# A two-layer trunk on one core of Trainium2: three of seven out-projection operands kept as plain values, weight differences in order of use, conditioning loads tied to their pairs

## The chip, the cores and the metric

The kernel runs on one core of a Trainium2 chip. A core has five engines with a queue of instructions each: TensorE (PE) multiplies matrices, VectorE (DVE), ScalarE (ACT) and GpSimd (POOL) work on tiles, SyncE (SP) here only starts DMA transfers. Each queue runs in its order; engines wait for one another through semaphores. The order within a queue is fixed when the program is built, by a scheduler that places the instructions by readiness and by the order in which the code emits them. The metric is the device time of one execution in microseconds, as the median of repeated runs.

## The reference

A trunk of two layers on 1024 positions of width 1024, fp32. Layer 0 mixes by gated DeltaNet and stick-breaking attention, layer 1 by retention; each mixer and each SwiGLU feed-forward has an RMS norm, modulated by rows that are computed from a conditioning vector (adaLN). What the change touches is the last two of these:

```python
for l in range(DEPTH):
    mod = (c_act @ ada_w[l] + ada_b[l])[:, None, :]
    sh_m, sc_m, gt_m, sh_f, sc_f, gt_f = jnp.split(mod, 6, axis=-1)
    h = rms_norm(x, norm_mix[l]) * (1 + sc_m) + sh_m
    ...
    x = x + gt_m * y
    h = rms_norm(x, norm_ffn[l]) * (1 + sc_f) + sh_f
    gu = h @ ffn_w_in[l]
    g, u = gu[..., :2816], gu[..., 2816:]
    x = x + gt_f * ((silu(g) * u) @ ffn_w_out[l])
```

## The kernel before

Activations are held transposed, as eight tiles of 128x1024 in fp32 (`xs`). A product of two fp32 matrices is made of three TensorE products: each operand is split into a high part (`hi`, a cast on ACT) and a low part (`lo`, value minus `hi`, a subtraction on DVE or POOL), and hi·hi, lo·hi and hi·lo are summed.

**The seven-product scheme.** `wino` (L1280) computes a pair of 128-wide output blocks by the Strassen–Winograd scheme: seven products in place of eight. The activation side has the operands A11, A12, A22, S1, S2, S3, S4 (quarters of the input and sums of them), the weight side B11, B21, B22, T1, T2, T3, T4. One product is 12 matmuls of 128x512 (4 slices of the contraction, three for hi and lo). `main` runs the pairs; in each the order of the products is A11·B11 (`m1`), S2·T2 and S3·T3 (`m67`), S1·T1 (`m5`), A22·T4 (`m4`), A12·B21 (`m2`), S4·B22 (`m3`). After each product the function `step(n, nm)` of the caller runs, which emits other work there. The weights of a pair come as two raw tiles of 128x1024 by SP (`w_load`, L127, two buffers). `prep_a` splits the first (L1297, L1298); `prep_b` (L1303–1327) makes the differences on the raw tiles in place (L1317, L1318, L1321, L1322) and splits B22, T2, T1, T3, T4 (L1319/1320, L1325/1326). Sums of the results are made at L1378–1398. The scheme serves three places: the feed-forward's input projection (pairs 0 to 21 of a feed-forward), the first 16 of 22 hidden blocks of its output projection (pairs 22 to 29, two groups `p` of four pairs) and the retention's input projection (16 pairs). Of a feed-forward's first seven pairs the products A11 and A12 run early, beside the norm; what they gave goes to DRAM (`early_d`) and is read back one pair ahead (`reload`), with the silu of the gate behind it (L1466).

**Operands of the output projection.** While pairs 0 to 15 run, `FfnParts` (L1459) takes the hidden values of each second pair and emits, one step per product, the sums S1 to S4 and the two parts of all seven operands, and stores these in DRAM (`hop_d`) by DMAs that POOL starts (L1502, L1503, L1505). The output projection reads them back: `HidOps.load` (L1519) starts, behind each product of pair 21 (for p = 0) and of pair 25 (p = 1), the four transfers of 512 KB of the operand that has just become free (two halves, two parts). With two layers that makes four such load stages of 28 transfers. All run in SP's queue, in order; at most eight are under way. The sums of the output pairs are added to the residual at L1545.

**adaLN rows in the background.** The rows of layer 1 are dot products of a weight tile with the conditioning vector, one DVE instruction each. `ada1` (L1678) does 32 half rows for the mixer during layer 0's feed-forward: every third product it multiplies the tile that was asked for last (L1684) and asks for the next, into one tile. `ada2` (L1768) does 32 rows of 512 KB during the retention's projection, at S2, S1 and A12 of each pair, with three tiles, multiplying (L1776) what was asked for two steps ago. Both are tied to the place in the program only by their buffers: the scheduler is free to put them earlier where these are free.

**Retention's v rows.** Before the retention's projection, `v_rows` (L1734) computes the values v with plain products; their results are copied out of PSUM by ACT (L1748, tiles `rvt`, two buffers) and stored by SP (L1749, `rv_d`).

## Time and profile before

| | us |
|---|---|
| median of three runs | 3076.23 (3074.4 to 3081.41) |
| profiled execution | 3077.01 |
| its span, first to last instruction | 3074.9 |
| PE busy | 2948.5 |
| DVE busy | 2219.3 |
| ACT busy | 1297.0 |
| POOL busy | 555.2 |
| mean granted clock of TensorE | 0.992 |

The profile is that of one execution. Lines of groups have the line, engine, operation, output and input tiles with shapes, the count, then busy time and mean length in ns, then the idle time of the engine ahead of them and what ended it. Lines of waits have the engine and line that waited, what for, the total, how often, and the longest. The windows give for a stretch of time how long each engine was busy, with the number of its instructions in brackets; for PE this number is a measure of progress, since nearly all matmuls are of the same size. `raw` is an unsplit weight tile, `whi`/`wlo` and `thi`/`tlo` are split weights, `mA`, `mB`, `mD`, `mE` are PSUM results of the scheme, `u`, `c` and `sg` are sums in SBUF, `x` stands for any of the eight tiles `xs`.

### The profile page before, as it was taken

What the parts mean: (1) busy time and instruction counts of PE and PEld (TensorE: products, weight loads), DVE (VectorE), ACT (ScalarE), POOL (GpSimd) and SP (SyncE); (2) the same over time, 40 slices, a digit from 0 to 9 for tenths busy, and PEclk for the clock granted to TensorE, in tenths of its full rate; (3) what the DMA queues carried; (4) which work ended last, traced back from release to release, by engine and by line L of the source; (5) the groups of instructions that cost most, each with busy time, mean ns of one, the idle gap of its engine ahead of it and who ended that gap; (6) DMA issues with size and microseconds to landing.
All of it is one profiled execution on the core that took longest, in us unless ns stands there. A gap on an engine that the chain in (4) does not pass through costs nothing.

```text
span 3074.9 us, 41844 instructions
## 1 busy us (share of the span) xinstructions
PE 2948.5 (96%) x15640; PEld 2343.1 (76%) x15640; DVE 2219.3 (72%) x3377; ACT 1297.0 (42%) x2155; POOL 555.2 (18%) x574
## 2 busy tenths in 40 slices
PE   8999999999989999999989999999999899999999
PEld 4777787867767878877768788887777678888777
DVE  6677866699798887666786555578866988775665
ACT  5444556788664433222352333333233644432221
POOL 1222221367332211000130000001111322110000
PEclk9999999999999999999999999999999999999999
DMA  6333333420156555355469333362212565454553
GB/s 228 125 117 114 128 97 100 140 94 28 62 189 222 202 188 200 139 215 214 144 232 316 130 110 110 112 234 99 104 49 83 175 206 176 152 192 167 216 202 130
DMA packets 167163, 471.93 MB, mean 153 GB/s; under 512 B 20912, under 2 KB 29872, under 8 KB 166448
## 3 DMA queue, kind: packets, MB, share of 16 engines
q1 hardware_dynamic: 148432, 409.54, 38.5%
q0 software_dynamic: 18064, 58.93, 5.2%
q8 instruction: 123, 2.02, 0.3%
q10 hardware_dynamic: 464, 0.79, 0.1%
q14 instruction: 80, 0.66, 0.1%
HBM read 337.58 MB, written 131.60 MB: 153 GB/s over the span
## 4 chain that ended last, share of the span: by engine, by line
PE 64%; DVE 18%; DMA 10%; issue 4%; ACT 3%; POOL 1%; SPq 0%; DVEq 0%; ACTq 0%; POOLq 0%
PE mB L1334 3%; PE mB L1336 3%; PE ops L161 3%; PE mA L1336 3%; PE mB L1335 3%; PE mA L1334 3%; PE mA L1335 3%; PE mD L1334 3%; PE mD L1335 3%; PE mD L1336 3%; PE ops L162 3%; PE ops L163 3%; PE rvps L1745 3%; PE gps L161 2%; PE gps L163 2%
## 5 line engine op out<-in xcount | busy, mean ns | idle before, releaser
L141 ACT CAST whi<-raw 128x1024 fp32r<-128x1024 f32 x126 | 132.1, 1051 | 201.0 <-PE ops L162 85.7
L1505 POOL DMA_DIRECT2D hop_d<-x x224 | 121.1, 543 | 462.1 <-ACT x L1502 300.9
L309 DVE SCALAR_TENSOR_TENSOR x<-ops,mod,x 128x512 f32<-128x512 f32 x160 | 119.5, 747 | 105.1 <-PE ops L163 104.7
L142 DVE TENSOR_TENSOR wlo<-raw,whi 128x1024 fp32r<-128x1024 f32 x124 | 163.1, 1316 | 32.1 <-ACT whi L141 29.9
L1325 ACT CAST thi<-raw 128x512 fp32r<-128x512 f32 x228 | 130.4, 620 | 112.2 <-DVE raw L1321 96.4
L161 PE MATMUL gps<-hh,whi 128*128 128x512 f32 x352 | 166.2, 472 | 0.0
L1326 DVE TENSOR_TENSOR tlo<-raw,thi 128x512 fp32r<-128x512 f32 x228 | 149.7, 706 | 2.8 <-ACT thi L1325 2.8
L1297 ACT CAST whi<-raw 128x1024 fp32r<-128x1024 f32 x62 | 65.3, 1054 | 194.2 <-DMA raw<-in_w_fout_dram 96.2
L1012 POOL TENSOR_TENSOR sl<-ab,sh 128x512 fp32r<-128x512 f32 (+1 forms) x80 | 116.4, 1456 | 149.9 <-ACT ab L996 83.0
L163 PE MATMUL gps<-hh,wlo 128*128 128x512 f32 x352 | 140.1, 398 | 0.0
L1319 ACT CAST whi<-raw 128x512 fp32r<-128x512 f32 x76 | 47.3, 623 | 219.6 <-PE mA L1335 183.9
L162 PE MATMUL gps<-hl,whi 128*128 128x512 f32 x352 | 139.7, 397 | 0.0
L1298 DVE TENSOR_TENSOR wlo<-raw,whi 128x1024 fp32r<-128x1024 f32 x62 | 77.3, 1246 | 85.7 <-ACT whi L1297 85.7
L161 PE MATMUL ops<-osh,whi 128*128 128x512 f32 x320 | 127.6, 403 | 10.1 <-DVE x L309 8.1
L162 PE MATMUL ops<-osl,whi 128*128 128x512 f32 x320 | 127.5, 399 | 4.3 <-DVE osl L1949 3.7
L1334 PE MATMUL mD<-S4h,whi 128*128 128x512 f32 x304 | 119.9, 394 | 9.2 <-DVE c L1387 9.2
L1334 PE MATMUL mA<-A12h,whi 128*128 128x512 f32 x304 | 120.3, 396 | 7.4 <-ACT u L1346 7.4
L1334 PE MATMUL mA<-A11h,whi 128*128 128x512 f32 x304 | 119.9, 394 | 7.4 <-ACT whi L1297 3.7
L163 PE MATMUL ops<-osh,wlo 128*128 128x512 f32 x320 | 125.7, 394 | 0.0
L1335 PE MATMUL mE<-A,thi 128*128 128x512 f32 x304 | 119.2, 392 | 6.0 <-DMA A<-hop_d 6.0
L1336 PE MATMUL mA<-A11h,wlo 128*128 128x512 f32 x304 | 120.6, 398 | 4.2 <-DVE wlo L1298 2.9
L1336 PE MATMUL mB<-S2h,tlo 128*128 128x512 f32 x304 | 119.3, 392 | 5.0 <-DVE tlo L1326 5.0
(451 smaller groups left out, 8990.4 us busy)
## 6 DMA issues: line engine op xcount, KB each, us to landing
hop_d<-x POOLq DMA_DIRECT2D x224, 256.0 KB, 3.7
raw<-in_w_fin_dram SPq DMA_DIRECT2D x102, 512.0 KB, 4.4
raw<-in_w_rin_dram SPq DMA_DIRECT2D x64, 512.0 KB, 4.3
raw<-in_w_fout_dram SPq DMA_DIRECT2D x52, 512.0 KB, 4.5
gth<-in_adaT_dram SPq DMA_DIRECT2D x64, 256.0 KB, 2.9
x<-in_adaT_dram SPq DMA_DIRECT2D x32, 512.0 KB, 5.6
raw<-in_w_hyb_dram SPq DMA_DIRECT2D x28, 512.0 KB, 3.7
x_d<-x SPq DMA_DIRECT2D x24, 512.0 KB, 2.9
```

What stands on the lines that cost most here:

```text
L141: A.copy(hi, raw)
L142: eng.tensor_tensor(lo, raw, hi.bitcast(F32), op=ALU.subtract)
L161: PE.matmul(ps, whi, xh, start=start, stop=False)
L162: PE.matmul(ps, whi, xl, start=False, stop=False)
L163: PE.matmul(ps, wlo, xh, start=False, stop=stop)
L309: V.scalar_tensor_tensor(xs[dt][:, sl], ps, gts(dt), xs[dt][:, sl], op0=ALU.mult, op1=ALU.add)
L1325: A.copy(hi, t)
L1326: e.tensor_tensor(lo, t, f32(hi), op=ALU.subtract)
L1334: PE.matmul(ps, w[0][:, c], xh[k], start=(start and k == 0), stop=False, skip_group_check=True)
L1335: PE.matmul(ps, w[0][:, c], xl[k], start=False, stop=False, skip_group_check=True)
L1336: PE.matmul(ps, w[1][:, c], xh[k], start=False, stop=(k == 3), skip_group_check=True)
L1505: G.dma_start(hop_d[self.l][p, m, i][:, j * HT:j * HT + HT], t.bitcast(F32))
```

## The change

1. S1, A22 and A12 are stored as plain values: one POOL transfer in place of two for each, and no cast and subtraction in `FfnParts`. At the load two transfers of 512 KB in place of four bring the values to the place of the low part, and `HidOps.split` makes the high part (cast on ACT) and the low part in place (subtraction on DVE), behind the products A11 (for S1), S2 (for A22) and S3 (for A12) of pair 22 or 26.
2. `prep_b` emits B22 and its parts, T2 and its parts, T3's parts, T4, T1's parts, T4's parts, in place of all differences first.
3. `pin` copies one column of the current pair's B22 into the adaLN tile on ACT ahead of each adaLN load, so that the load has to come behind it. `ada1` has two tiles, and multiplies what was asked for two steps ago; its two loads of the conditioning vector are at steps 0 and 17.

```diff
-    def wino(name, ops_of, fpa, npairs, ne, ev_of, step=lambda n, nm: None):
+    def wino(name, ops_of, fpa, npairs, ne, ev_of, step=lambda n, nm, w: None):
...
-            A.copy(w["B22"][0], b22)
-            EB[2].tensor_tensor(w["B22"][1], b22, f32(w["B22"][0]), op=ALU.subtract)
-            EB[3].tensor_tensor(b22, b22, b11, op=ALU.subtract)
-            EB[4].tensor_tensor(b21, b21, b22, op=ALU.subtract)
-            for nm, t, e in (("T2", b22, EB[5]), ("T1", b11, EB[6]), ("T3", b12, EB[7]), ("T4", b21, EB[8])):
+            def parts(nm, t, e):
                 hi, lo = w[nm]
                 A.copy(hi, t)
                 e.tensor_tensor(lo, t, f32(hi), op=ALU.subtract)
+
+            EB[0].tensor_tensor(b11, b12, b11, op=ALU.subtract)
+            EB[1].tensor_tensor(b12, b22, b12, op=ALU.subtract)
+            parts("B22", b22, EB[2])
+            EB[3].tensor_tensor(b22, b22, b11, op=ALU.subtract)
+            parts("T2", b22, EB[5])
+            parts("T3", b12, EB[7])
+            EB[4].tensor_tensor(b21, b21, b22, op=ALU.subtract)
+            parts("T1", b11, EB[6])
+            parts("T4", b21, EB[8])
...
+    def pin(t, w):
+
+        A.copy(t[:, 0:1], w["B22"][0][:, 0:1].bitcast(F32))
...
-            self.steps += [parts(*a) for a in (("S1", s1), ("A11", a11), ("A12", a12), ("A22", a22), ("S3", s3), ("S2", s2), ("S4", s4))]
+            def values():
+                for nm, v in (("S1", s1), ("A22", a22), ("A12", a12)):
+                    G.dma_start(hop_d[self.l][p, MATS.index(nm), 0][:, j * HT:j * HT + HT], v)
+            self.steps.append(values)
+            self.steps += [parts(*a) for a in (("A11", a11), ("S3", s3), ("S2", s2), ("S4", s4))]
...
+    WHOLE = ("S1", "A22", "A12")
...
             for j in range(2):
                 for i in range(2):
-                    nc.sync.dma_start(self.t[nm][i][j].bitcast(F32), src[i][:, j * T:j * T + T])
+                    if nm in WHOLE:
+                        if i == 0:
+                            nc.sync.dma_start(self.t[nm][1][j].bitcast(F32), src[0][:, j * T:j * T + T])
+                    else:
+                        nc.sync.dma_start(self.t[nm][i][j].bitcast(F32), src[i][:, j * T:j * T + T])
+
+        def split(self, nm):
+            for hi, lo in zip(*self.t[nm]):
+                A.copy(hi, lo.bitcast(F32))
+                V.tensor_tensor(lo, lo.bitcast(F32), hi.bitcast(F32), op=ALU.subtract)
...
+        AT = dict(A11="S1", S2="A22", S3="A12")
+
+        def step(n, nm, w):
             if n >= 21 and (n - 21) % 4 == 0 and (n - 21) // 4 < NWP:
                 ho[(n - 21) // 4].load(nm)
+            if n >= 22 and (n - 22) % 4 == 0 and nm in AT:
+                ho[(n - 22) // 4].split(AT[nm])
...
     def ada1(at):
-        def f():
-            acb, w = (xs[0][:, i * HT:i * HT + HT] for i in range(2))
-            if at:
-                i, ch, dt = aq1[at - 1]
-                j = 48 + ch * 8 + dt
+        def f(wt):
+            place = lambda i: xs[i // 2][:, (i % 2) * HT:(i % 2) * HT + HT]
+            acb, ws = place(0), (place(1), place(2 + MATS.index("S1")))
+            if at > 1:
+                i, ch, dt = aq1[at - 2]
+                j, w = 48 + ch * 8 + dt, ws[at % 2]
                 V.scalar_tensor_tensor(w, w, 1.0, acb, op0=ALU.mult, op1=ALU.mult, accum_out=(mod, mod2)[i][:, j:j + 1])
...
+            if at in (0, 17):
+                nc.sync.dma_start(acb, cb_d[:, at // 17 * HT:at // 17 * HT + HT])
             if at < len(aq1):
                 i, ch, dt = aq1[at]
-                if (ch, dt) == (1, 0):
-                    nc.sync.dma_start(acb, cb_d[:, i * HT:i * HT + HT])
-                nc.sync.dma_start(w, adaT[48 + ch * 8 + dt][:, i * HT:i * HT + HT])
+                pin(ws[at % 2], wt)
+                nc.sync.dma_start(ws[at % 2], adaT[48 + ch * 8 + dt][:, i * HT:i * HT + HT])
...
-    def ada2(n, nm):
+    def ada2(n, nm, wt):
...
             if at < len(aq2):
                 ch, dt = aq2[at]
+                pin(xs[1 + (at + 2) % 3], wt)
                 nc.sync.dma_start(xs[1 + (at + 2) % 3], adaT[48 + ch * 8 + dt])
```

In the changed file lines stand a little lower: the difference of B12 and B11 is L1322, that of B22 and B12 L1323, all casts and subtractions of the T parts L1319 and L1320, the sums L1378, L1380, L1387, L1393, L1398 are L1382, L1384, L1391, L1397, L1402, the silu of a reloaded gate is L1474, the pin L1460, a plain load L1545, the new split L1551 (ACT) and L1552 (DVE), the residual add L1567, and the adaLN products are L1709 and L1802.

Where the scheduler puts these instructions is seen in the engines' order. First DVE at the first load stage (pair 22 of layer 0, from the sum that takes its product S3 on; `raw`, `whi`, `wlo` are weights of pair 23); before:

```order
L1380 TENSOR_TENSOR u_12362<-u_12348,mB 128x512 [waits DVE_49,PE_49]
L1298 TENSOR_TENSOR wlo<-raw,whi 128x1024 [waits DMAHW7_49,Activation_49]
L1317 TENSOR_TENSOR raw<-raw 128x512 [waits DMAHW0_49,DVE_49]
L1318 TENSOR_TENSOR raw<-raw 128x512 [waits DVE_49]
L1387 TENSOR_TENSOR c_12404<-u_12362,mD 128x512 [waits DMAHW5_49,PE_49]
L1545 SCALAR_TENSOR_TENSOR x_6317<-mA,mod,x_6317 128x512 [waits PE_49]
L1545 SCALAR_TENSOR_TENSOR x_6318<-c_12404,mod,x_6318 128x512 [waits DMASW4_49,DVE_49]
L1320 TENSOR_TENSOR wlo<-raw,whi 128x512 [waits Activation_49]
L1326 TENSOR_TENSOR wlo<-raw,whi 128x512 [waits Activation_49]
```

and with the change:

```order
L1384 TENSOR_TENSOR u_12320<-u_12302,mB 128x512 [waits DVE_49,PE_49]
L1552 TENSOR_TENSOR S1l<-S1l,S1h 128x1024 [waits DMAHW7_49,Activation_49]
L1552 TENSOR_TENSOR S1l<-S1l,S1h 128x1024 [waits DMAHW0_49,Activation_49]
L1552 TENSOR_TENSOR A_12225<-A_12225 128x1024 [waits DMAHW1_49,Activation_49]
L1552 TENSOR_TENSOR A_12225<-A_12225 128x1024 [waits DMAHW2_49,Activation_49]
L1298 TENSOR_TENSOR wlo<-raw,whi 128x1024 [waits DMAHW3_49,Activation_49]
L1322 TENSOR_TENSOR raw<-raw 128x512 [waits DMAHW4_49,DVE_49]
L1323 TENSOR_TENSOR raw<-raw 128x512 [waits DVE_49]
L1552 TENSOR_TENSOR A12l<-A12l,A12h 128x1024 [waits DMAHW5_49,Activation_49]
L1391 TENSOR_TENSOR c_12370<-u_12320,mD 128x512 [waits DMAHW7_49,PE_49]
L1552 TENSOR_TENSOR A12l<-A12l,A12h 128x1024 [waits DMAHW6_49,Activation_49]
```

Six new subtractions stand there. The first stands behind the sum L1384 (L1380 before); the split of the next pair's raw tile (L1298) and its differences (L1322, L1323; L1317, L1318 before), which followed that sum at once, stand behind four of them.

Second, ACT in layer 0's feed-forward, one of the first pairs, whose gate `sg` is read back from DRAM; before:

```order
L1319 CAST whi<-raw 128x512 [waits DMAHW1_49]
L1502 CAST x_6318<-x_6322 128x512 [waits DVE_49]
L1502 CAST x_6321<-x_6324 128x512 [waits DVE_49]
L1466 ACTIVATE sg<-sg 128x512 [waits DMAHW3_49,Activation_49]
L1325 CAST whi<-raw 128x512 [waits DMAHW7_49,DVE_49]
L1325 CAST thi_9510<-raw 128x512 [waits DVE_49,PE_49,Activation_49]
L1325 CAST thi_9512<-raw 128x512 [waits PE_49,Activation_49]
L1325 CAST thi_9516<-raw 128x512 [waits DVE_49,PE_49,Activation_49]
```

and with the change:

```order
L1319 CAST whi<-raw 128x512 [waits DMAHW5_49]
L1460 COPY x_6319<-whi 128x1 [waits Activation_49]
L1510 CAST x_6321<-x_6324 128x512 [waits DVE_49]
L1319 CAST whi<-raw 128x512 [waits DMAHW4_49,DVE_49]
L1474 ACTIVATE sg<-sg 128x512 [waits DMAHW6_49]
L1319 CAST thi_9512<-raw 128x512 [waits DVE_49,PE_49]
L1319 CAST thi_9514<-raw 128x512 [waits PE_49]
L1319 CAST thi_9518<-raw 128x512 [waits DVE_49,PE_49]
```

The T1 cast (the second `whi`) stood behind the silu of the reloaded `sg`; it stands ahead of it now, and a pin has come in behind the B22 cast.

Third, SP in the retention's v rows, which loads their weights (`raw`) and stores their results (`rv_d`); before:

```order
L1783 DMA x_6320<-in_adaT_dram 128x1024 [waits DMAHW0_49,DVE_49]
L131 DMA raw<-in_w_rin_dram 128x1024 [waits DMAHW6_49,DMAHW1_49,DVE_49]
L1783 DMA x_6318<-in_adaT_dram 128x1024 [waits DMAHW2_49,DVE_49]
L131 DMA raw<-in_w_rin_dram 128x1024 [waits DMAHW7_49,DMAHW3_49,DVE_49]
L1783 DMA x_6319<-in_adaT_dram 128x1024 [waits DMAHW4_49]
L1749 DMA rv_d<-rvt 128x512 [waits DMAHW5_49,Activation_49]
L1749 DMA rv_d<-rvt 128x512 [waits Activation_49]
L131 DMA raw<-in_w_rin_dram 128x1024 [waits DMAHW1_49,DVE_49]
L1783 DMA x_6320<-in_adaT_dram 128x1024 [waits DMAHW0_49]
L1749 DMA rv_d<-rvt 128x512 [waits Activation_49]
L1749 DMA rv_d<-rvt 128x512 [waits DMAHW2_49,Activation_49]
```

and with the change:

```order
L131 DMA raw<-in_w_rin_dram 128x1024 [waits DMAHW2_49,DVE_49]
L131 DMA raw<-in_w_rin_dram 128x1024 [waits DMAHW4_49,DVE_49]
L131 DMA raw<-in_w_rin_dram 128x1024 [waits DMAHW0_49,DVE_49]
L1775 DMA rv_d<-rvt 128x512 [waits DMAHW3_49,Activation_49]
L131 DMA raw<-in_w_rin_dram 128x1024 [waits DMAHW1_49,DVE_49]
L1775 DMA rv_d<-rvt 128x512 [waits DMAHW5_49,Activation_49]
L1775 DMA rv_d<-rvt 128x512 [waits DMAHW6_49,Activation_49]
L1775 DMA rv_d<-rvt 128x512 [waits DMAHW7_49,Activation_49]
L131 DMA raw<-in_w_rin_dram 128x1024 [waits DMAHW2_49,DVE_49]
```

The adaLN loads (512 KB each) are gone from between the stores; all but the first stand behind the last of these, among the loads of the 16 pairs.

More of the change, by code (lines that the diff above doesn't have):

```diff
@@ L1336, in prod @@
                 PE.matmul(ps, w[1][:, c], xh[k], start=False, stop=(k == 3), skip_group_check=True)
-            step(n, nm)
+            step(n, nm, pairs[n])
         bank = lambda nm: pf[0].tile([P, HT], F32, tag="w", name=nm)
@@ L1637, in proj_ffn @@
         spare = list(spare)
-        def step(n, nm):
-            if n < 0:
-                return
+        AT = dict(A11="S1", S2="A22", S3="A12")
+        def step(n, nm, w):
             if n >= 21 and (n - 21) % 4 == 0 and (n - 21) // 4 < NWP:
                 ho[(n - 21) // 4].load(nm)
+            if n >= 22 and (n - 22) % 4 == 0 and nm in AT:
+                ho[(n - 22) // 4].split(AT[nm])
             if fp.steps:
@@ L1686, in f @@
                     ada_finish(1, ch)
+            if at in (0, 17):
+                nc.sync.dma_start(acb, cb_d[:, at // 17 * HT:at // 17 * HT + HT])
             if at < len(aq1):
                 i, ch, dt = aq1[at]
-                if (ch, dt) == (1, 0):
-                    nc.sync.dma_start(acb, cb_d[:, i * HT:i * HT + HT])
-                nc.sync.dma_start(w, adaT[48 + ch * 8 + dt][:, i * HT:i * HT + HT])
+                pin(ws[at % 2], wt)
+                nc.sync.dma_start(ws[at % 2], adaT[48 + ch * 8 + dt][:, i * HT:i * HT + HT])
         return f
-    proj_ffn(0, gt0, os_, lambda: load(0), [ada1(at) for at in range(len(aq1) + 1)])
+    proj_ffn(0, gt0, os_, lambda: load(0), [ada1(at) for at in range(len(aq1) + 2)])
     ret = {}
```

4 lines of the change are left out of this document (1 added, 3 removed).

## The prediction

> **What bounds the kernel now.** First the page: busy shares, and the chain that ended last.
>
> ```profile
> PE 2948.5 (96%) x15640; PEld 2343.1 (76%) x15640; DVE 2219.3 (72%) x3377; ACT 1297.0 (42%) x2155; POOL 555.2 (18%) x574
> PE 64%; DVE 18%; DMA 10%; issue 4%; ACT 3%; POOL 1%; SPq 0%; DVEq 0%; ACTq 0%; POOLq 0%
> ```
>
> TensorE is the bound; what can be won are the stretches in which it isn't fed. So next the windows of 25 us: a window at full pace holds 112 matmuls (1350:1375), 25/112 = 0.2232 us each, and each one missing is a loss of that size. The columns are PE, PEld, DVE, ACT, POOL busy (with counts), clock, DMA share, GB/s.
>
> ```profile
> 875.00:900.00 25.00, 23.57 (x102) 18.57 (x101) 24.90 (x30) 18.95 (x30) 8.66 (x6) 1.00 0.62 204
> 900.00:925.00 25.00, 19.43 (x82) 14.63 (x80) 23.80 (x30) 10.94 (x18) 7.00 (x3) 1.00 0.52 172
> 925.00:950.00 25.00, 23.85 (x98) 19.65 (x99) 21.16 (x39) 11.27 (x19) 3.61 (x7) 0.93 0.62 201
> 950.00:975.00 25.00, 21.54 (x95) 17.17 (x94) 21.31 (x38) 8.66 (x15) 5.48 (x11) 1.00 0.59 200
> 1300.00:1325.00 25.00, 22.69 (x95) 17.12 (x94) 11.04 (x18) 4.54 (x8) 0.00 (x0) 1.00 1.03 412
> 1325.00:1350.00 25.00, 22.13 (x93) 16.73 (x92) 17.87 (x26) 5.49 (x8) 0.00 (x0) 1.00 0.58 221
> 1350.00:1375.00 25.00, 25.00 (x112) 20.68 (x111) 17.67 (x27) 7.28 (x12) 0.00 (x0) 1.00 0.12 43
> 1400.00:1425.00 25.00, 20.97 (x72) 14.32 (x70) 9.38 (x14) 3.42 (x6) 0.00 (x0) 0.86 0.76 303
> 1575.00:1600.00 25.00, 21.17 (x91) 16.55 (x90) 24.84 (x26) 11.47 (x15) 9.83 (x3) 1.00 0.70 224
> 1600.00:1625.00 25.00, 22.48 (x99) 18.27 (x99) 15.61 (x23) 6.57 (x8) 0.00 (x0) 1.00 0.93 312
> 1700.00:1725.00 25.00, 22.17 (x97) 17.72 (x96) 15.34 (x15) 10.84 (x16) 5.31 (x2) 1.00 0.34 108
> 1750.00:1775.00 25.00, 25.00 (x112) 20.69 (x111) 12.50 (x19) 9.13 (x14) 0.00 (x0) 1.00 0.35 126
> 2500.00:2525.00 25.00, 23.70 (x103) 19.00 (x102) 23.45 (x40) 10.58 (x18) 6.49 (x12) 1.00 0.68 228
> 2525.00:2550.00 25.00, 22.88 (x101) 18.52 (x100) 21.49 (x35) 11.65 (x20) 6.08 (x12) 1.00 0.62 214
> 2825.00:2850.00 25.00, 24.05 (x103) 18.67 (x101) 12.07 (x18) 5.58 (x9) 0.00 (x0) 1.00 1.03 411
> 2850.00:2875.00 25.00, 20.75 (x84) 15.20 (x85) 14.53 (x21) 5.49 (x8) 0.00 (x0) 1.00 0.74 288
> 2925.00:2950.00 25.00, 20.97 (x85) 15.29 (x84) 8.99 (x13) 2.78 (x4) 0.00 (x0) 1.00 0.92 367
> ```
>
> Four places that the change touches lose time:
> - The **four load stages** of the out-projections: 36 matmuls missing in 1300–1350 (8.0 us), 40 in 1400–1425 (8.9), 37 in 2825–2875 (8.3), 27 in 2925–2950 (6.0), 31.2 us in all. DMA share and GB/s are at their highest there: the queue is full.
> - **Feed-forward of layer 0, norm and first pairs** (875–975): 71 missing, 15.8 us, DVE at 21 to 25 of 25.
> - **Layer 1's first pairs** (2500–2550): 20 missing, 4.5 us.
> - **Retention's v rows** (1575–1625, 1700–1725): 49 missing, 10.9 us; DMA share up to 0.93.
>
> **The load stages.** The two longest waits of TensorE in the second one, 1400–1434 (total, times, longest), and from the first one a row of the chain, the sum on DVE at the S1 product, and this product's first two matmuls.
>
> ```profile
> PE mE L1335 <- DMA A<-hop_d: 1.5, 2, 0.8
> PE mA L1334 <- ACT whi L1297: 0.9, 1, 0.9
> ```
> ```profile
> 1315.19 10.18 DMA raw<-in_w_fout_dram
> ```
> ```profile
> 1316.21 0.69 DVE L1380 TENSOR_TENSOR u<-u,mB 128x512 f32<-128x512 f32 x1 [1.98 <-PE mB L1336]
> ```
> ```profile
> 1316.01 0.39 PE L1334 MATMUL mD<-S1h,whi 128*128 128x512 f32 x1
> 1316.44 0.50 PE L1335 MATMUL mD<-S1l,whi 128*128 128x512 f32 x1
> ```
>
> A 512 KB load takes 10.18 us with eight in flight, so one lands every 1.27 us, and TensorE needs an operand (four of them, 5.1 us) every 2.72 us (12 matmuls). The queue is the bound. The change takes 6 of 28 transfers out of a stage: 6 × 1.27 = 7.6 us, 24 and 30.5 us in all. In return come, per stage, six casts and six subtractions of 128x1024. Their like:
>
> ```profile
> L1297 ACT CAST whi<-raw 128x1024 fp32r<-128x1024 f32 x62 | 65.3, 1054 | 194.2 <-DMA raw<-in_w_fout_dram 96.2
> ...
> L1298 DVE TENSOR_TENSOR wlo<-raw,whi 128x1024 fp32r<-128x1024 f32 x62 | 77.3, 1246 | 85.7 <-ACT whi L1297 85.7
> ```
>
> 6 × 1.05 = 6.3 us on ACT and 6 × 1.25 = 7.5 us on DVE, in stretches where these have 4.5 and 11 of 25 us to do: room in sum, not at every moment. The walk of stage one: the raw tile lands at 1325.37; eight transfers ahead of it is S1's first, at 1325.37 − 8 × 1.27 = 1315.2. S1's first piece takes this place. Its cast ends at 1316.3; its subtraction stands behind the sum L1380 (L1384 in the changed file), which ends at 1316.9, and ends at 1318.15. The second S1 matmul, at 1316.44 before, comes then; without any wait it would stand one step behind the first (1316.01 + 0.22), so this is 1.9 us of wait. From there DVE's subtractions come at 1319.4, 1320.6 and 1321.9 and TensorE needs them at about 1319.5, 1320.9 and 1322.2: no more wait. The raw tile has four transfers fewer ahead of it, so it lands at 1320.3 instead of 1325.4, and its halves are ready at 1323.2, when A11·B11 begins (1323.3). For the T sums behind it I add 0.6. Loss 2.5 instead of 8.0: **5.5**, and the third stage (8.3) likewise 5.8. In the second and fourth residual adds stand between the splits on DVE, three of 128x512 ahead of what TensorE needs, some 0.7 us each (as L1380); I add 2.2 for them: losses 4.7, gains 4.2 and 1.3. **Sum 16.8 us.** Bounds: −1 per stage (each wait is replaced by one on DVE, and the sums behind it slip) and 31.2, all of the loss. I take the walk, since every duration in it has a row.
>
> The Trainium skill ("DMA: Bandwidth & Descriptors", Where 436 GB/s comes from) has HBM to SBUF bound at about 358 GB/s a core; this trace moves 412 and 411 in the two fullest windows, so the measurement decides. By the page's figure a transfer would be 1.46 us and the 24 be worth an estimated 35 us of queue instead of 30.5.
>
> **The producing side.** Per layer 24 casts, 24 subtractions and 24 POOL transfers go. They lay in pairs 0 to 15 beside a full TensorE except at the start, so I count them in the next term only.
>
> **Layer 0's feed-forward.** The adaLN product (L1684) and its kind in retention, what was saved on the producing side, and the waits of TensorE in 905–1240:
>
> ```profile
> L1503 DVE TENSOR_TENSOR x<-x,x 128x512 fp32r<-128x512 f32 x112 | 76.9, 690 | 5.6 <-ACT x L1502 5.6
> ...
> L1776 DVE SCALAR_TENSOR_TENSOR x<-x,x 128x1024 f32<-128x1024 f32 x32 | 41.3, 1293 | 28.3 <-DMA x<-in_adaT_dram 28.1
> ...
> L1684 DVE SCALAR_TENSOR_TENSOR x<-x 128x512 f32<-128x512 f32 x32 | 24.3, 758 | 15.1 <-DMA x<-in_adaT_dram 15.1
> ```
> ```profile
> PE mD L1334 <- DVE c L1387: 5.8, 3, 2.4
> PE mB L1334 <- ACT thi L1325: 3.1, 4, 1.8
> PE mB L1336 <- DVE tlo L1326: 1.9, 5, 0.5
> ```
> ```profile
> 954.55 0.63 ACT L1466 ACTIVATE sg<-sg 128x512 f32<-128x512 f32 x1 [3.27 <-DMA sg<-early_d]
> ```
>
> DVE stands 15.1 us before adaLN products for loads that were asked for one step ahead into one tile; with two tiles they are asked for two steps ahead, and four products leave the norm stage, where DVE is full. The T1 cast stands behind a silu that waited 3.27 us for its reload; in the changed order it is ahead of it. Both feed the three waits for c (5.8 us), which I count as gone, with half of the 5.0 on thi and tlo: **8 us**. Bounds 3 (the silu alone) and 13. In **layer 1** only the T1 order and the three subtractions (0.69 each) change: **2 us** of 4.5; bounds 0 and 4.5.
>
> **Retention.** 32 loads of 512 KB, 32 × 1.27 = 40.6 us of queue, and 32 products leave the v rows for pairs 0 to 10 of the projection behind. In the v rows TensorE waited so:
>
> ```profile
> PE rvps L1745 <- ACT rvt L1748: 6.0, 5, 2.5
> PE mA L1334 <- ACT rvt L1748: 2.6, 1, 2.6
> ```
>
> The evictions rvt have two buffers and wait for their store, which waited behind adaLN loads. The 6.0 go: **6 us**; the 2.6 at the end of the stage stay. Bounds 3 and 9. In the projection DVE has 12.5 of 25 us to do (1750:1775), 9.5 per pair of 19.05 us; three products add 3 × 1.29 = 3.9: 70%. Price 0, hidden by DVE's idle half; up to 6 if half a microsecond a pair is exposed. The **pins** are casts of one column:
>
> ```profile
> L420 ACT ACTIVATE mod<-shp,vecs 128x1 f32<-128x1 f32 x8 | 2.1, 262 | 13.5 <-DVE modA L418 13.5
> ```
>
> 64 × 0.26 = 17 us on an engine that is busy 42%: nothing, if none waits (see the third rival).
>
> **Sum.** 16.8 + 8 + 2 + 6 = 32.8 us. The profiled execution took 3077.0 us (span 3074.9 and 2.1 around it), 0.8 above the median of 3076.2. 3077.0 − 32.8 = 3044.2; I say **3045 us**.
>
> **Rivals.**
> 1. *The split takes the transfer's place.* TensorE then waits for cast and subtraction, 2.3 us behind each landing, wherever ACT or DVE is at another row. For it: L1380 ahead of the first split, the residual adds in stages two and four. Against: 11 of 25 us of DVE. If the four stages give 5 in place of 16.8: 3077 − 21 = 3056.
> 2. *Only the loads pay*: DVE stays full in 875–925 with other work and the stores of rvt wait for raw weights instead. 3077 − 17 = 3060.
> 3. *Slower: the pin holds ACT.* A pin may only write when the product that used its tile is done, and it stands behind the T1 cast, ahead of the silu and the T2 cast. If that product still waits for its load (before, 15.1 us over 10 waits, 1.5 each), ACT waits, T2 waits, TensorE waits, in some 17 pairs of layer 0 and 11 of retention: 28 × 1.5 = 42 us, against 25 of the other terms: 3094. It decides from 0.9 us a pair on. Against it: loads are asked for two steps of three products ahead, 2 × 3 × 2.72 = 16 us, and even with eight in flight one took 10.18.
> 4. *No change*: the queue isn't the bound and the waits only change names: 3077. The 412 GB/s speak against it.
> 5. *The clock.* In 1400–1425 it was 0.86, though no wait on the list there passed 0.9 us: some 7 us at half speed, 3.5 lost. If that comes again beside the new wait of 1.9 us: 3048.
>
> The Trainium skill ("TensorE: Matmul & The Clock Gate", Part 1, What's actually happening) halves the clock after an idle window of about 3.4 us. By that rule rival 5 could not come, nor could the row's 0.86 have; the trace speaks against it here, so the rival stays.
>
> **How the numbers follow.** Forecast with rival 5 inside it (3030 to 3052) 0.58; rival 1 0.16; rival 2 0.14; rival 3 0.06; rival 4 0.06. All lower bounds of layer 0, layer 1 and v rows, with 8 from the loads, give 3077 − 14 = 3063; the upper ones with 22 from the loads give 3077 − 48 = 3029. Range 3030 to 3064. A measurement tells about 0.2% (6 us; the runs shown lie 7 apart): faster 0.88, same 0.06, slower 0.06.
>
> **What would show it.** In the load stages: DMA share below 1 behind S1, S1's second matmul waiting about 1.9 us for the new subtraction, no wait for raw at L1297's successor; windows back above 100. In 875–975 more than 20 matmuls more, no wait for c. In 1575–1700 no wait of rvps for rvt over 1 us; 1750–1950 still 112. Wrong if ACT idles before pins, or if the S1, A22 and A12 products each wait for their split.

## The result, and the profile after

The changed kernel takes 3040.68 us (median of four runs, 3040.25 to 3041.19) beside 3075.32 for the kernel before: a ratio of 0.9885 with a 95% interval of 0.9868 to 0.9902. The forecast was 3045 with a range of 3030 to 3064. The profiled execution's span went from 3074.9 to 3038.6 us.

Busy shares and chain of the page after:

```profile
PE 2939.2 (97%) x15640; PEld 2347.6 (77%) x15640; DVE 2214.9 (73%) x3353; ACT 1301.9 (43%) x2195; POOL 526.3 (17%) x526
...
PE 72%; DVE 16%; DMA 5%; issue 3%; ACT 2%; POOL 1%; SPq 0%; DVEq 0%; ACTq 0%; POOLq 0%
```

DMA's share of the chain has halved, from 10% to 5%; DVE and ACT are as busy as before. The transfers were made fewer (446.75 MB moved, 471.93 before); TensorE, DVE and ACT have nearly as much work as before, and wait less. The windows of the same four places, which come earlier on the clock by what was gained until then:

```profile
875.00:900.00 25.00, 24.02 (x105) 19.09 (x104) 24.38 (x26) 20.01 (x30) 9.50 (x6) 1.00 0.56 184
900.00:925.00 25.00, 19.53 (x83) 14.89 (x82) 23.14 (x27) 11.74 (x22) 6.40 (x3) 1.00 0.49 163
925.00:950.00 25.00, 25.00 (x105) 20.45 (x104) 22.97 (x42) 9.87 (x19) 4.93 (x9) 0.93 0.65 218
950.00:975.00 25.00, 24.75 (x109) 20.18 (x108) 22.72 (x41) 9.93 (x19) 4.51 (x9) 1.00 0.71 235
1300.00:1325.00 25.00, 23.54 (x101) 18.39 (x100) 19.65 (x27) 11.34 (x14) 0.00 (x0) 1.00 0.78 312
1325.00:1350.00 25.00, 25.00 (x112) 20.69 (x111) 18.20 (x28) 5.49 (x8) 0.00 (x0) 1.00 0.25 85
1375.00:1400.00 25.00, 22.77 (x97) 17.62 (x96) 18.91 (x25) 10.74 (x14) 0.00 (x0) 1.00 0.85 338
1400.00:1425.00 25.00, 25.00 (x111) 20.24 (x110) 19.77 (x30) 7.15 (x13) 0.00 (x0) 1.00 0.24 80
1575.00:1600.00 25.00, 25.00 (x112) 20.71 (x111) 6.12 (x5) 8.52 (x11) 0.00 (x0) 1.00 0.48 152
1600.00:1625.00 25.00, 25.00 (x112) 20.71 (x111) 4.91 (x5) 8.49 (x11) 0.00 (x0) 1.00 0.51 166
1750.00:1775.00 25.00, 25.00 (x112) 20.67 (x112) 18.38 (x30) 9.78 (x19) 0.00 (x0) 1.00 0.66 218
2800.00:2825.00 25.00, 23.31 (x103) 18.96 (x102) 18.26 (x26) 10.84 (x15) 0.00 (x0) 1.00 1.03 412
```

The first load stage now misses 11 matmuls in its two windows where 36 were missing, the second 16 where 40 were. The v rows run at 112 in the windows shown, and the retention's projection (1750:1775) has the adaLN products on DVE (18.4 us in place of 12.5) and still runs at 112. The waits of TensorE in the first and in the second load stage:

```profile
PE mD L1339 <- DVE S1l L1552: 1.4, 1, 1.4
```
```profile
PE mD L1339 <- DVE S1l L1552: 1.7, 1, 1.7
PE mE L1339 <- DVE A L1552: 0.3, 1, 0.3
PE mA L1339 <- DVE A12l L1552: 0.2, 1, 0.2
```

All waits for a landing are gone. What stands in their place is above all one wait for S1's subtraction, at the place that the forecast named (1.7 us in the third and the fourth stage too):

```profile
1306.66 0.69 DVE L1384 TENSOR_TENSOR u<-u,mB 128x512 f32<-128x512 f32 x1 [1.97 <-PE mB L1340]
1307.26 2.35 DVE L1552 TENSOR_TENSOR S1l<-S1l,S1h 128x1024 fp32r<-128x1024 f32 x2
```
```profile
1308.54 0.50 PE L1339 MATMUL mD<-S1l,whi 128*128 128x512 f32 x1 [1.43 <-DVE S1l L1552]
```

To compare whole stages, I took the time between the same two matmuls by count (both programs have 15,640) in each kernel and subtracted that of the kernel before. The stages are cut at matmuls that run at the times given in the kernel before; minus is a gain in us. The experiments e1 to e10 stand beside the change, each from its one profiled execution; "rest" scatters by up to 4 us between executions, so a row says something from about 1 us on where it is a load stage or the v rows, and from 2 or 3 in the others. Where a stage still has the full queue it scatters more: e10, with the transfers of the kernel before, stands 0.2 to 1.6 us behind it in the load stages. The span here is that from the first matmul to the last.

```
stage (times of before)         after     e1     e2     e3     e4     e5     e6     e7     e8     e9    e10
layer 0: first pairs 870-1060    -5.3   -4.2   +5.0   -5.1   +4.4   -4.3   -4.1   -5.8   -5.1   -0.1   -4.9
layer 0: later pairs 1060-1200   -4.6   -4.6   -4.6   -4.6   -2.0   -4.6   -4.6   -4.6   -4.6   -4.6   -4.5
load stage 1         1316-1350   -5.8   -5.7   -6.1   -5.7   -4.9   -7.0   -0.8   -7.7   -0.9   -6.4   +1.6
load stage 2         1400-1437   -5.5   -5.5   -5.5   -5.5   -5.5   -4.7   +0.8   -9.1   -2.9   -5.2   +0.2
v rows               1600-1735   -4.9   +0.9   -5.0   -5.1   +2.9   -5.1   -5.0   -5.1   -5.1   -4.8   -5.1
retention projection 1735-2000   +0.8   -0.0   -0.1   +0.5   -0.1   -0.0   +0.6   +0.5   -0.1   +0.3   +0.3
layer 1: to pair 10  2340-2600   -2.8   -2.5   -3.3   -2.4   -1.4   -2.0   -2.5   -2.9   -2.7   -2.5   +0.1
load stage 3         2840-2878   -5.6   -5.6   -5.6   -5.6   -5.6   -5.9   +1.1   -7.6   -1.2   -5.6   +1.5
load stage 4         2925-2962   -2.6   -2.7   -2.6   -2.7   -2.6   -3.4   +2.9   -6.2   -0.1   -2.4   +1.0
rest                             +0.1   -0.1   +0.6   +1.1   +0.5   -0.4   +3.7   +2.5   -2.4   -1.9   +1.6
span                            -36.2  -30.1  -27.2  -35.0  -14.3  -37.4   -7.9  -46.0  -25.1  -33.3   -8.2
```

The change gained 19.5 us in the four load stages, 9.9 in layer 0's feed-forward, 4.9 in the v rows and 2.8 in layer 1.

Part of some rows is TensorE's clock. In the load stages and v rows of these traces it falls to half for 3.4 or 6.8 us at a time (granted clock 0.50 from 1410.8 to 1417.6 in the kernel before, 15 matmuls where a full pace has 30), which costs half of that while TensorE is busy: some 3.4 us in the second load stage of the kernel before, which are part of the 5.5 gained there. The change, e1, e2, e3, e7 and e9 have no such stretch in these rows. e4 has one of 3.4 us in the first load stage and two in the v rows, e5 one in the second load stage, e6 one in the first, second and fourth, e8 one in each of the four, and e10 one in the first and the fourth and one of 6.8 us in the second.

### The profile page after: what moved, and what is told of

Same layout as the page of the kernel before. It is cut to its first block, busy times and chain, and to the rows that moved or that the text cites. A ratio compares the mean times of both kernels' runs of the same rounds, so it can differ in the third digit from the quotient of the medians.

```text
span 3038.6 us, 41660 instructions
## 1 busy us (share of the span) xinstructions
PE 2939.2 (97%) x15640; PEld 2347.6 (77%) x15640; DVE 2214.9 (73%) x3353; ACT 1301.9 (43%) x2195; POOL 526.3 (17%) x526
## 2 busy tenths in 40 slices
DMA packets 159866, 446.75 MB, mean 147 GB/s; under 512 B 19760, under 2 KB 28720, under 8 KB 159152
## 4 chain that ended last, share of the span: by engine, by line
PE 72%; DVE 16%; DMA 5%; issue 3%; ACT 2%; POOL 1%; SPq 0%; DVEq 0%; ACTq 0%; POOLq 0%
PE rvps L1771 4%; PE mD L1339 4%; PE mD L1340 4%; PE mD L1338 4%; PE mA L1338 4%; PE mA L1339 4%; PE mA L1340 4%; PE mB L1340 4%; PE mB L1339 4%; PE mB L1338 4%; PE ops L161 3%; PE ops L162 3%; PE ops L163 3%; PE gps L161 3%; PE gps L163 2%
## 5 line engine op out<-in xcount | busy, mean ns | idle before, releaser
L1319 ACT CAST whi<-raw 128x512 fp32r<-128x512 f32 x152 | 88.5, 620 | 224.2 <-PE mA L1339 192.2
L1319 ACT CAST thi<-raw 128x512 fp32r<-128x512 f32 x228 | 129.5, 619 | 109.8 <-DVE raw L1325 81.6
L1320 DVE TENSOR_TENSOR tlo<-raw,thi 128x512 fp32r<-128x512 f32 x228 | 150.2, 704 | 2.8 <-ACT thi L1319 2.8
L1320 DVE TENSOR_TENSOR wlo<-raw,whi 128x512 fp32r<-128x512 f32 x152 | 98.9, 686 | 53.6 <-ACT whi L1319 53.6
L1298 DVE TENSOR_TENSOR wlo<-raw,whi 128x1024 fp32r<-128x1024 f32 x62 | 77.2, 1246 | 68.7 <-ACT whi L1297 68.6
L1339 PE MATMUL mD<-S1l,whi 128*128 128x512 f32 x304 | 118.8, 391 | 6.5 <-DVE S1l L1552 6.5
L1513 POOL DMA_DIRECT2D hop_d<-x x128 | 69.1, 541 | 314.0 <-ACT x L1510 203.8
L1486 ACT ACTIVATE u<-u 128x512 f32<-128x512 f32 x44 | 27.8, 633 | 221.1 <-DVE u L1402 221.1
```

What stands on the lines that cost most here:

```text
L1319: A.copy(hi, t)
L1320: e.tensor_tensor(lo, t, f32(hi), op=ALU.subtract)
L1339: PE.matmul(ps, w[0][:, c], xl[k], start=False, stop=False, skip_group_check=True)
```

## The experiments

The kernel before was timed again beside each group of experiments: 3076.48 us beside e1 to e4, 3073.44 beside e5 to e8, 3078.01 beside e9 and e10. Medians of different groups can therefore differ by a few us without a difference between the kernels; the ratios allow for that.

### One part undone, one part alone (e1 to e4)

**e1: no pin in the retention's projection.**

```diff
-                pin(xs[1 + (at + 2) % 3], wt)
```

> The changed kernel without the pin ahead of the adaLN loads of the retention projection; nothing else. The scheduler then puts these 32 loads and products back among the v rows. Theory (the pin's only effect is to keep 32 x 512 KB out of the queue while the v rows store their results): the v rows lose the 4 to 5 us that they gained, the projection behind stays at full pace, about 3045 us. Rival (the v rows gained by the other parts, or the pins cost something in the projection): 3041 or less.

Measured: 3044.46 us (3044.25 to 3046.12), a ratio to the kernel before of 0.9901 [0.9887, 0.9916]. The v rows lose 5.8 us against the change, all other rows stay within 1.1. TensorE's waits from 1550 to 1740 are those of before again:

```profile
PE rvps L1771 <- ACT rvt L1774: 6.4, 4, 2.8
PE mA L1338 <- ACT rvt L1774: 2.6, 1, 2.6
```

So the gain of the v rows is the pin's, and the pin costs the projection nothing that can be told.

**e2: no pin in layer 0's feed-forward.**

```diff
-                pin(ws[at % 2], wt)
```

> The changed kernel without the pin ahead of the adaLN loads of layer 0's feed-forward; two tiles and two steps ahead stay. Theory (the pin keeps the first products out of the norm stage, where DVE is full, and the order of the pairs behind follows from two tiles): 2 to 4 us are lost in the norm and the first pairs and nothing after them, about 3043 to 3045. Rival (two tiles and the work taken from DVE by the plain values do it all): 3041.

Measured: 3050.02 us (3048.12 to 3051.08), 0.9918 [0.9903, 0.9932]: 9.3 us worse than the change, more than twice the 2 to 4 of the theory. Without the pin the first pairs are slower than in the kernel before (+5.0). The adaLN products on DVE from 875 to 1060 say why:

```profile
L1709 DVE SCALAR_TENSOR_TENSOR x<-x 128x512 f32<-128x512 f32 x16 | 13.2, 823 | 2.1 <-DMA x<-in_adaT_dram 2.1
L1709 DVE SCALAR_TENSOR_TENSOR x<-x,x 128x512 f32<-128x512 f32 x16 | 10.9, 684 | 2.9 <-DMA x<-in_adaT_dram 2.9
```

All 32 products run there, in the stretch where DVE is fullest; with the pin 18 do. Without the pin, two tiles let the scheduler take the whole row of products forward.

**e3: the old order of the weight differences.** `prep_b` as in the kernel before.

```diff
-            parts("B22", b22, EB[2])
-            EB[3].tensor_tensor(b22, b22, b11, op=ALU.subtract)
-            parts("T2", b22, EB[5])
...
+            for nm, t, e in (("T2", b22, EB[5]), ("T1", b11, EB[6]), ("T3", b12, EB[7]), ("T4", b21, EB[8])):
```

> The changed kernel with the weight differences emitted in the old order. Theory (the T1 cast stands behind the silu of the reloaded gate again): one wait of about 2.4 us comes back in the first pairs of each layer, about 3045; in steady pairs nothing. Rival (the order decides nothing, since the scheduler orders by readiness): 3041.

Measured: 3043.07 us (3041.6 to 3044.39), 0.9896 [0.9881, 0.991]. The 2.4 us to the change are under the 0.2% that can be told, and in the stages in question nothing is lost (−9.7 beside −9.9 in layer 0, −2.4 beside −2.8 in layer 1). The rival holds: beside the other parts of the change, the order in which the differences are emitted decides nothing. The new order alone, on the kernel before, was not run.

**e4: the three plain operands alone, on the kernel before.** Point 1 of the change with nothing else:

```diff
+    WHOLE = ("S1", "A22", "A12")
...
+            self.steps.append(values)
+            self.steps += [parts(*a) for a in (("A11", a11), ("S3", s3), ("S2", s2), ("S4", s4))]
...
+            if n >= 22 and (n - 22) % 4 == 0 and nm in AT:
+                ho[(n - 22) // 4].split(AT[nm])
```

> The kernel before with the three plain operands alone (stores, loads and splits), old order, no pins, one adaLN tile. Theory (the parts add up): the four load stages gain what they gained in the full change, 19 us, and the first pairs 1 to 3 us from three subtractions less, about 3053 to 3056. Rival (the load stages also need the new order of the weight differences, since splits and differences share DVE): load stages gain under 15 us, about 3060.

Measured: 3061.42 us (3058.47 to 3062.16), 0.9952 [0.9936, 0.9969]. The load stages gain 18.6 of the change's 19.5, with the old order and without pins, so they stand by themselves. But the rest is not what the theory had: the first pairs of layer 0 lose 4.4 and the v rows 2.9. In the first pairs, with work gone from DVE, the scheduler drew 22 adaLN products ahead of 1060, where it had 17, and DVE waits 11.2 us there for their loads in place of 6.0: the room that part 1 made was filled with the products that hurt there. In the v rows the 32 products and the waits for `rvt` are those of before (6.1 and 2.6 us beside 6.0 and 2.6); what differs is two stretches at half clock, 0.93 in two windows that stood at 1.00:

```profile
1600.00:1625.00 25.00, 24.87 (x103) 20.04 (x102) 15.52 (x22) 6.71 (x9) 0.00 (x0) 0.93 0.92 311
1700.00:1725.00 25.00, 22.41 (x92) 17.90 (x91) 17.39 (x20) 9.92 (x17) 3.43 (x2) 0.93 0.28 94
```

So outside the load stages part 1 needs the pins; that the pins do not need part 1 is seen in e10.

### What the load stages gain by (e5, e6, e8)

**e6: the splits stay, the queue is as long as before.**

```diff
-                        if i == 0:
-                            nc.sync.dma_start(self.t[nm][1][j].bitcast(F32), src[0][:, j * T:j * T + T])
+                        nc.sync.dma_start(self.t[nm][i][j].bitcast(F32), src[0][:, j * T:j * T + T])
```

> The changed kernel with 28 transfers again in each load stage: the plain value is also loaded into the place of the high part, which the cast then writes over. Stores, splits and everything else stay. Theory (the gain of the load stages is queue time, 1.27 us for each of the 6 transfers that went): all of it goes and the split comes on top, so at least 8 us are lost per stage as before, 3060 to 3070. Rival (the gain came from fewer stores and from moved instructions, not from the queue): 3041 to 3045.

Measured: 3067.01 us (3059.53 to 3069.16), 0.9972 [0.9961, 0.9984]. The four stages go from −19.5 to +4.0: 23.5 us for 24 transfers. The first load stage's window:

```profile
1300.00:1325.00 25.00, 20.27 (x76) 14.25 (x74) 13.88 (x17) 8.53 (x10) 0.00 (x0) 0.93 1.03 409
```

The queue is at 409 GB/s again, and the splits come on top, each behind one more transfer. About 5 of the 23.5 us are half clock (0.93 in this window). The gain was queue time, with the half clock that came with the longer waits, and nothing else of the change brought it.

**e5: the queue stays short, the splits go.** Both parts of S1, A22 and A12 are read from the plain values, so the output projections of the first 16 hidden blocks give other numbers.

```diff
-            if n >= 22 and (n - 22) % 4 == 0 and nm in AT:
-                ho[(n - 22) // 4].split(AT[nm])
...
         def get(self, nm, part):
+            part = 1 if nm in WHOLE else part
```

> The changed kernel without the splits of S1, A22 and A12 after the load: both parts of these three operands are read from the plain values, so the first 16 hidden blocks of the output projections come out as other numbers. Transfers, matmuls and everything else stay. Theory (what is left of the loss in the load stages, 2.0 to 2.9 us each in the profile after, is the split behind the landing): the waits for S1l, A and A12l go, four times about 2 us, 3033 us. Rival (the queue is still the bound and the waits would be for the landing in its place): 3039 to 3041.

Measured: 3039.89 us (3037.78 to 3042.72), 0.9888 [0.9873, 0.9902], no different from the change. The wait for S1l is gone, as it must be, and the first stage gains 1.2 us; but in the second TensorE now waits 2.3 us, where before the wait was hidden behind that of S1:

```profile
PE mA L1340 <- DVE wlo L1298: 2.3, 1, 2.3
```
```profile
1390.43 0.69 DVE L1402 TENSOR_TENSOR u<-u,mE 128x512 f32<-128x512 f32 x1 [1.25 <-PE mE L1340]
1391.15 0.75 DVE L1568 SCALAR_TENSOR_TENSOR x<-u,mod,x 128x512 f32<-128x512 f32 x1
1391.82 1.22 DVE L1298 TENSOR_TENSOR wlo<-raw,whi 128x1024 fp32r<-128x1024 f32 x1
```

The raw tile of the next pair stands behind the operands in the queue, and its split was put behind a sum and a residual add. Neither theory had this row. Behind this wait the clock was at half for 3.4 us (0.93 in 1375 to 1400), some 1.7 us. Taking the splits away is worth 1.5 us in the four stages, about 3 without that stretch, where the theory had 8: the next wait in line takes their place.

**e8: S4 in place of S1 among the three.**

```diff
-    WHOLE = ("S1", "A22", "A12")
+    WHOLE = ("A22", "A12", "S4")
...
-        AT = dict(A11="S1", S2="A22", S3="A12")
+        AT = dict(S2="A22", S3="A12", S1="S4")
```

> The changed kernel with S4 in place of S1 among the three plain operands: also 22 transfers per stage, but the two that go stand at the end of the queue instead of ahead of A22. Theory (each operand is late by what stands ahead of it in the queue): S1 waits for its landing (about 1.2 us), A22 for landing and split (about 2), so a stage loses 3 to 4 us in place of 2 to 3, 3043 to 3047. Rival (any three operands do, only the sum of the transfers counts): 3039 to 3041.

Measured: 3052.27 us (3051.43 to 3053.37), 0.9928 [0.9913, 0.9942]. As many transfers as in the change, but 14.5 us of the 19.5 are lost (−5.0 in four stages). The first stage's waits:

```profile
PE mD L1339 <- DMA S1l<-hop_d: 1.6, 2, 0.8
PE mE L1338 <- ACT A L1551: 0.9, 1, 0.9
PE mE L1339 <- DVE A L1552: 0.8, 1, 0.8
```

The direction is the theory's; the time is 11.6 us above the change where the theory had 2 to 6. Nearly half of the 14.5 is the clock: each of the four stages has one stretch of 3.4 us at half, 1.7 us each, as in the first:

```profile
1300.00:1325.00 25.00, 21.62 (x80) 15.31 (x78) 13.76 (x16) 9.08 (x11) 0.00 (x0) 0.93 0.75 300
```

A transfer saved behind the point at which TensorE waits brings little; S1's two are worth so much because A22, A12, S4 and the raw tile stand behind them.

### A11 too (e7), and the two halves of the adaLN part (e9, e10)

**e7: A11 plain as well**, split behind product S1 of pair 21 or 25, 20 transfers a stage.

```diff
-    WHOLE = ("S1", "A22", "A12")
+    WHOLE = ("S1", "A22", "A12", "A11")
...
+            if n >= 21 and (n - 21) % 4 == 0 and (n - 21) // 4 < NWP and nm == "S1":
+                ho[(n - 21) // 4].split("A11")
```

> The changed kernel with A11 kept as plain values too, split behind product S1 of pair 21 or 25: 20 transfers per stage. Theory (S1's split is late because S1 lands just when the sum of S3 is due on DVE; two transfers fewer ahead of it bring it 2.5 us earlier and its subtractions then stand ahead of that sum): the wait of 1.4 to 1.7 us goes in all four stages, and each layer's first pairs have a subtraction less: 3033 to 3036. Rival (two more casts and subtractions of 128x1024 per stage crowd ACT and DVE and other waits take its place): 3040 to 3046.

Measured: 3028.36 us (3026.9 to 3030.23), 0.985 [0.9835, 0.9865], 12 us faster than the change by the medians, 10 by the profiled spans, and better than the theory had it. The four stages gain 30.5 us, nearly all of the 31.2 that were missing in the windows of before. S1 lands earlier and its subtractions run ahead of the sum:

```profile
1304.80 0.69 DVE L1382 TENSOR_TENSOR u<-u,mB 128x512 f32<-128x512 f32 x1 [1.78 <-issue]
1305.41 2.36 DVE L1552 TENSOR_TENSOR S1l<-S1l,S1h 128x1024 fp32r<-128x1024 f32 x2
1307.68 0.68 DVE L1384 TENSOR_TENSOR u<-u,mB 128x512 f32<-128x512 f32 x1
```
```profile
1375.00:1400.00 25.00, 25.00 (x112) 20.45 (x111) 21.98 (x30) 13.01 (x17) 0.00 (x0) 1.00 0.69 275
```

Between 1295 and 1420 no wait of TensorE is on the list any more. DVE has 22 of 25 us to do there, so a fifth operand would have little room.

**e10: the pins alone, on the kernel before** (one tile, one step ahead, in layer 0; three tiles in the retention, as there).

```diff
+                pin(w, wt)
                 nc.sync.dma_start(w, adaT[48 + ch * 8 + dt][:, i * HT:i * HT + HT])
...
+                pin(xs[1 + (at + 2) % 3], wt)
                 nc.sync.dma_start(xs[1 + (at + 2) % 3], adaT[48 + ch * 8 + dt])
```

> The kernel before with the pins alone, in layer 0's feed-forward (one tile, one step ahead) and in the retention projection; stores, loads, order of differences as before. Theory (the pin acts by itself): the v rows gain 5 us, the first pairs of layer 0 gain 3 to 5, the load stages nothing: 3064 to 3068 beside 3073 to 3076 of before. Rival (in layer 0 the pin is only needed where two tiles let the products crowd, before it was one product in three already): the v rows alone, 3069 to 3071.

Measured: 3065.81 us (3058.33 to 3068.32), 0.995 [0.9931, 0.9968]. The profile is that of the slowest of the five runs. In it layer 0 gains 9.4 us and the v rows 5.1, as much as the whole change does there, with the old order, one tile and all 224 stores. So the pins do it by themselves, though the number of products ahead of 1060 (17) is that of the kernel before. What they move is the load. SP's issues in the kernel before, and ACT's silu behind them (shown in the prediction, 954.55, after 3.27 us of waiting):

```profile
946.44 0.33 SPq L1691 DMA_DIRECT2D x<-in_adaT_dram  x1
948.85 0.33 SPq L1364 DMA_DIRECT2D sg<-early_d  x1
```

and with the pins alone:

```profile
948.91 0.33 SPq L1364 DMA_DIRECT2D sg<-early_d  x1
949.29 0.45 SPq L1364 DMA_DIRECT2D u<-early_d  x1
950.10 0.33 SPq L1696 DMA_DIRECT2D x<-in_adaT_dram  x1
```
```profile
951.92 0.64 ACT L1470 ACTIVATE sg<-sg 128x512 f32<-128x512 f32 x1 [0.58 <-DMA sg<-early_d]
952.46 0.60 ACT L1325 CAST whi<-raw 128x512 fp32r<-128x512 f32 x1
```

The pin hangs on the cast of B22, late in the pair; so the adaLN load is asked for behind the reload of the gate and not ahead of it, the gate is there 2.6 us earlier, and the T1 cast, still behind the silu in this order, no longer waits. By the same count of matmuls, the stretch from 950 to 960 of the kernel before gains 2.5 us with the pins alone and 2.7 with the change: about half of what the first pairs gain. The later pairs of the kernel before lost their 4.6 us at another place: a product that waited for its load just ahead of the split of B22.

```profile
1094.40 0.69 DVE L1684 SCALAR_TENSOR_TENSOR x<-x 128x512 f32<-128x512 f32 x1 [1.57 <-DMA x<-in_adaT_dram]
1095.02 0.08 DVE L1684 DVE_READ_ACCUMULATOR x<-x 128x1 f32 x1
1095.02 0.69 DVE L1320 TENSOR_TENSOR wlo<-raw,whi 128x512 fp32r<-128x512 f32 x1
```

With the pins alone the product still waits for its load in the same pair:

```profile
1088.39 0.69 DVE L1688 SCALAR_TENSOR_TENSOR x<-x 128x512 f32<-128x512 f32 x1 [1.22 <-DMA x<-in_adaT_dram]
1089.01 0.08 DVE L1688 DVE_READ_ACCUMULATOR x<-x 128x1 f32 x1
1089.01 0.69 DVE L1484 TENSOR_TENSOR x<-c,u 128x512 f32<-128x512 f32 x1
1089.61 0.69 DVE L1320 TENSOR_TENSOR wlo<-raw,whi 128x512 fp32r<-128x512 f32 x1
```

But the load was asked for earlier in the pair. Take the last matmul of A11h and whi in the A11·B11 product as the mark, which is the same matmul by count: it runs at 1096.41 in the kernel before and at 1092.96 here. The load was asked for 5.6 us ahead of it there and 7.9 here, the split of B22 starts 1.4 us ahead of it there and 3.35 here, and TensorE no longer waits.

**e9: the change with one tile in layer 0 again**, one step ahead; the pin stays.

```diff
-            acb, ws = place(0), (place(1), place(2 + MATS.index("S1")))
-            if at > 1:
-                i, ch, dt = aq1[at - 2]
+            acb, w = (xs[0][:, i * HT:i * HT + HT] for i in range(2))
+            if at:
+                i, ch, dt = aq1[at - 1]
```

> The changed kernel with one tile for the adaLN rows of layer 0's feed-forward again, asked for one step ahead; the pin stays. Theory (what the steady pairs, 1060 to 1200 of before, gained, 4.65 us, comes from asking two steps ahead, since DVE no longer stands before a product for its load): about 4 us come back there, 3044 to 3046. Rival (the pin and its even pace of one product in three are enough, a load of 256 KB lands well within three products, 8 us): 3041.

Measured: 3045.91 us (3043.28 to 3047.27), 0.9896 [0.9878, 0.9913]. The later pairs keep their 4.6 us, so it was not the second tile that brought them. The first pairs lose 5.2 against the change; there DVE waits 6.6 us for adaLN loads. By the ratios the kernels do not differ: 0.9896 and 0.9885, each inside the interval of the other. The profiles differ by the 5.2 us in the first pairs, but e10 gains 4.9 there with one tile too, so it is not shown that this is the second tile's worth; what e9 lacks there stays open.

## Why the prediction was right, step by step

**The load stages** (16.8 forecast, 19.5 measured). The queue as the bound, the place and the kind of the new wait (S1's second matmul behind the sum of S3) were right. Counted as the forecast counted it, from one matmul to the next less one step, this wait was 1.7 us in the first stage and 1.85 in the others (listed as 1.4 and 1.7) for the 1.9. All that the stages still lose, counted in the same way, is 2.4, 3.6, 2.4 and 3.6 us, where the walk had 2.5, 4.7, 2.5 and 4.7. The 0.6 for the T sums came as 0.5 in the first and third: the two matmuls that wait for T1's parts, with the one behind each, come that much later than a full pace has them, in gaps too short for the list of waits:

```profile
1320.77 0.50 PE L1338 MATMUL mD<-S1h,whi 128*128 128x512 f32 x1
1321.76 0.50 PE L1340 MATMUL mD<-S1h,wlo 128*128 128x512 f32 x1
```

Mis-sized was the term for the residual adds in the second and fourth stages: 2.2 forecast, 1.1 measured (0.6 at a matmul of A22 and 0.5 at one of A12, listed as 0.3 and 0.2). The half clock in the second stage (0.86 in 1400:1425) did not come back beside the new wait: 1375 to 1425 stands at 1.00, which settles rival 5 for this execution; in e5 it came, behind a wait of 2.3 us. The Trainium skill ("TensorE: Matmul & The Clock Gate", Part 1, What's actually happening) ties the half clock to an idle window of about 3.4 us. In the second stage the kernel before has it with listed waits of 0.9 us at most, and the change has a longer wait, 1.7, and no half clock: by this trace it isn't the length of one wait that decides. What stands out is how many matmuls ran in the 3.4 us ahead, where a full pace has 15: 6 in the kernel before (1407.4 to 1410.8), 5 in e5 (1390.2 to 1393.6), 4 to 7 in the four stages of e8, but 8 around the wait of the change (1385.1 to 1388.5). Whether this number decides, no run tests.

**Rival 1**, that the split takes the transfer's place, is true of one wait in each stage and false of the sum. e5 shows more: without that wait the stages gain only 1.5 us further, because the raw tile's split is next.

**Layer 0's feed-forward** (8 forecast, 9.9 measured). The size was right and the reasons were largely not, so that the number came out near is in part luck. I gave the gain to the second tile, which ends DVE's 15.1 us of waiting for loads, to products that leave the norm stage, and to the T1 cast that stands ahead of the silu. e3 shows that beside the pins the order of T1 brings nothing; e10 has nearly all of the gain with one tile, with 9.0 us of DVE's waiting left and with T1 behind the silu. It is the pin, and at the places looked at it acts through SP's queue: the load goes behind the reload of the gate, or is asked for earlier in the pair, so that the weights' split is not late. The step that failed is the link from DVE's idle time and the T1 cast to the waits for c. The forecast counted all 5.8 us of these as gone and half of the 5.0 on thi and tlo; in the change 3.6 of the 5.8 stay, though no wait for c was one of the signs named,

```profile
PE mD L1338 <- DVE c L1391: 3.6, 3, 2.3
```

and of the 5.0 only 0.9 is left. DVE's idle time before a product was not TensorE's loss as such: of the 15.1 us, as far as these places show, only what made the weights' parts late cost anything.

**Layer 1** (2 forecast, 2.8 measured; e3 has 2.4 with the old order, e4 1.4, e10 none). By e3 it isn't the order; that it is the subtractions that went is not shown, since e4's 1.4 and these numbers lie within the scatter of this row.

**The v rows** (6 forecast, 4.9 measured) were right in mechanism: e1 gives the loss back. Less came than the 6.0 us of waits, since of those for `rvt` 2.4 us stayed, at the start of the v rows. **The projection's price** of 0 was right: 112 matmuls with DVE at 18.4 of 25 us.

**Rival 3**, the pin that holds ACT, did not come: in the trace of the change ACT waited 0.9 us in all before one pin, and a pin took 187 ns, not 262. **Rivals 2 and 4** are out, by the 9.9 and 4.9 us of layer 0 and the v rows and by the time.

Not foreseen was that the parts depend on one another: part 1 without the pins loses 4.4 us in the first pairs (e4), and two tiles without the pin lose 10.3 there against the change (e2); in both more adaLN products run in that stretch, 22 and 32 in place of 17 and 18.

## What to carry to other kernels

Where a stage is bound by its transfers, look for the operand that stands at the head of the queue and move its preparation to an engine with room: here two transfers fewer in each stage ahead of S1 brought 11 us more over four stages (e7), while six fewer behind it brought 5 in all, about 8 with the half clock taken out of both kernels (e8). Background work that a scheduler may place freely belongs tied to a place, by a cheap true dependency, before it is given more buffers; otherwise the buffers let it crowd where the engine is fullest, as in e2. And an idle time before an instruction is only a loss if what is queued behind it on that engine is what the bound engine waits for.

## What the runs showed that was not expected

The second load stage of the kernel before ran partly at half clock (0.86 over 25 us) though its listed waits were 0.9 us at most, and with the change, with one wait of 1.7 us in it, at 1.00. And at one place in layer 0 the silu of a reloaded gate came at 954.55 for a reload asked for at 948.85, with an adaLN load of 256 KB asked for 2.4 us ahead of it, and at 951.92 for a reload asked for at 948.91, with the adaLN load behind it (e10): 2.7 us apart, where 256 KB are 0.64 us of the queue at 1.27 us for 512 KB. Where the rest comes from is open; what else was under way in the two traces, stores among them, was not compared.
